# One transformer block on one core: gate and up products token-major, K chunks summed into PSUM, adaLN spans of 1024 columns, two store queues, a new order

## The chip, the cores and the metric

The kernel runs on one core of one Trainium2 chip. A core has TensorE (PE: matrix products into PSUM), VectorE (DVE), ScalarE (ACT), GpSimd (POOL) and SyncE (SP, which here only issues DMAs). The metric is the device time of one execution in microseconds. The kernel before takes 1223.05 us, the median of three runs (1222.06, 1223.05 and 1223.63).

## The reference, cut to what matters

One layer on 256 tokens of width 2048, all in fp32. `c` is one conditioning vector; the six adaLN vectors come out of one matrix-vector product with a 2048 x 12288 matrix.

```python
c_act = jax.nn.silu(c)
mod = c_act @ ada_w[l] + ada_b[l]
sh1, sc1, g1, sh2, sc2, g2 = jnp.split(mod, N_MOD, axis=-1)
h = rms_norm(x, mix_pre_g[l]) * (1.0 + sc1[:, None, :]) + sh1[:, None, :]
y = hybrid_mixer(h, w_in[l], conv_w[l], conv_b[l], conv_ln_g[l], conv_ln_b[l], w_out[l])
x = x + g1[:, None, :] * rms_norm(y, mix_post_g[l])
h = rms_norm(x, ffn_pre_g[l]) * (1.0 + sc2[:, None, :]) + sh2[:, None, :]
y = swiglu_ffn(h, w_gate[l], w_up[l], w_down[l])   # (silu(h @ w_gate) * (h @ w_up)) @ w_down
x = x + g2[:, None, :] * rms_norm(y, ffn_post_g[l])
```

`hybrid_mixer` multiplies h by `w_in` (2048 x 5120) to q, k, v (1024 columns each) and a, g (1024 each). u = a * sigmoid(g) goes through a causal depthwise convolution of width 31, a LayerNorm and silu; q, k, v through attention in 8 heads. Both halves side by side are multiplied by `w_out` (2048 x 2048). The FFN's inner width is 5632, in 11 groups of 512 columns.

## The kernel before, in words

**Weights.** Every weight matrix is streamed once from memory, in loads of 1 MiB (512 rows in four blocks of 128, by 512 columns) into five `raw` buffers, all issued on the SP queue (L604). Each half of a load (128 x 1024 numbers) is split in two: ScalarE rounds it to `wh` (L610), VectorE forms the rest `wl = raw - wh` (L611). There are five buffers of each. The activations are split likewise in a high and a low part, and each product is the sum of three matmuls: high x high, low weight x high, high weight x low.

**Two forms of product.** In the *side* form (L668 to L675) 128 weight columns are stationary and 256 tokens move, so it needs the high and low parts of both token tiles, and its result has channels on the partitions. In the *token-major* form (`mm`, L677 to L682) 128 tokens are stationary and 512 weight columns move; it needs one token tile alone, and its result has tokens on the partitions. A 1-MiB load takes 48 matmuls in the side form and 24 in the token-major one. Before, q, k, a, g, gate and up are of the side form, v, w_out and w_down token-major. The side form gives silu(gate)*up, called `hid`, in the layout in which w_down needs it as the stationary operand.

**PSUM and chunks.** Products accumulate in four `pa` tiles of 128 x 512, adaLN sums and transposes in four `pt` tiles. w_in, w_out, the first four gate/up groups and w_down run over their rows in several chunks. `put` (L709) copies a first chunk's result to SBUF with ScalarE (L715) and adds each later chunk's with VectorE (L717); the sum then lies in SBUF, from where sigmoid, silu, square and gain multiply read it.

**adaLN.** `ada` (L453) streams a span of columns: a load of 1 MiB is either eight matmuls of 256 columns or four of 512 on TensorE (L476), or as many multiply-adds on VectorE (L485 for the first, L487 for the rest). In the trace an fp32 matmul of this kind, of the sums (L518) and of the spreads (L512) counts twice, so that a load shows as x16 or x8 and one spread as x2. Then the 128 partial sums per column are summed by small matmuls with ones (L518), which gives shift and scale columns (L525, L529, L530), or spread over the partitions with a matmul of 512 columns for the two gates (L512), which are multiplied into the post-norm weights (L514). SC1, SH1 are the mixer's scale and shift, SC2, SH2 the FFN's, G1, G2 the gates. A span before has at most 512 columns. The first chunks of the mixer's input have two blocks of 128 channels (`chunks` 0, 2, 4, ...): `h_chunk` (L534) normalizes x (L544), transposes it on TensorE (L555), applies scale and shift (L561 on VectorE or L566 on ScalarE) and splits it (L576/L579 and L580).

**The rest.** The convolution (L759) is done per tap with ScalarE products (L788) that VectorE adds over all channels it covers (L791), for `nact` of the eight 128-channel blocks, and with multiply-adds on VectorE alone for the rest (L774). The LayerNorm (L804) uses TensorE for its sums (L811, L825). Between mixer and FFN, the residual sum is normalized and turned by TensorE transposes (L1119) in `h2_chunk` (L1113). At the end y is normalized, and VectorE adds it to x in eight pieces (L1186), each stored from the SP queue (L1187).

**Order.** A `Plan` gathers all steps as tasks with a cost, a priority (the table `pri`), dependences and buffers, and orders them once, when the program is built; each engine then executes its list in that order. The weight loads and the adaLN loads are two queues merged by the numbers `c_before`, `c_after`, `g1_before` and others. A step of `ada` marked as `a` in the table `mode` goes to TensorE or VectorE as the plan finds them free. Where the plan sees TensorE idle it puts in small *fill-in* matmuls of the identity (L422), whose results nobody reads. An engine whose next instruction waits holds all behind it.

Of the kernel before, what the change touches and what calls it, by code (L numbers as in the profile page):

```python
# [16 lines left out]
P = 128  # L17
# [271 lines left out]
class Job:  # L289
# [11 lines left out]
def block_kernel(ctx, tc, x, c, ada_w, ada_b, mix_pre_g, mix_post_g, w_in, conv_w, conv_b,  # L301
# [16 lines left out]
    hd_pool = ac_pool = t2_pool  # L318
    if CFG["uni"] < 2:
        hd_pool = Slots([sbt([P, 512], "hd%d" % i) for i in range(CFG["heads"])])  # L320
    if CFG["uni"] < 1:
        ac_pool = Slots([sbt([P, 512], "ac%d" % i) for i in range(CFG["acc"])])
    pri = CFG["pri"]
    br_pool = Slots([sbt([1, 512], "brow")])
# [14 lines left out]
        "w0": ("Q0", [P, 2, 2, 512], F32R), "w1": ("Q1", [P, 2, 2, 512], F32R), "w2": ("Q2", [P, 2, 2, 512], F32R),  # L339
        "conv": ("CV", [P, CT * (256 + HALO) + CT * 256], F32), "x1": ("CV", [P, NT, D], F32),  # L340
# [44 lines left out]
    nc.vector.memset(mhalf, -0.5)  # L385
    cpad = sbt([P, KB, 32], "cpad")
# [835 lines left out]
```

## Time and profile before

| | |
|---|---|
| median of three runs | 1223.05 us |
| the profiled execution's own time | 1223.58 us |
| its span in the profile | 1221.8 us |
| mean granted TensorE clock | 0.993 |
| busy: TensorE, VectorE, ScalarE, GpSimd | 98%, 72%, 49%, 1% |
| moved from memory | 304 MB, mean 251 GB/s |
| main matmuls: first, last | 34.5 us, 1212.2 us |
| last w_out product, first FFN product | 434.0 us, 449.0 us |

The span is the profiled execution from its first to its last instruction; 1.78 us of the execution's time lie outside it. In a row of the timeline stand the start, the duration, the engine, the line, the operation, what it writes and reads, the number of instructions joined in the row, and in brackets the idle time before it and who ended it. Durations of TensorE's matmuls overlap, so that their spacing is read from starts or from pieces of the chain. A row of the chain has a start, a duration, the engine, the tile and line. In the table of windows a stretch is followed by its length, the busy time and number of instructions of TensorE, its weight loads, VectorE, ScalarE and GpSimd, then the granted TensorE clock as a share of full speed, the DMA engines' share and the GB/s.

### The profile page before, as it was taken

The page shows a single profiled execution, that of the slowest core. Times are in us where ns is not written, and L with a number is a line of the kernel's source. Part 1 is how long each engine was busy: PE and PEld are TensorE (multiplying, and loading weights), DVE is VectorE, ACT ScalarE, POOL GpSimd, SP SyncE. Part 2 cuts the span into 40 slices and gives each one's busy share as a digit, 9 for nine tenths or more (in the row PEclk, how much of TensorE's full clock was granted, in tenths as well). Part 3 has the DMA queues.
Part 4 walks back from the last instruction along what each step waited for, and adds up shares of the span by engine and source line. Part 5 has one row for each costly group of instructions (what it writes and reads, how often), then busy time and mean ns, then how long its engine had stood idle before and what let it go on. Part 6 is the DMA issues. An engine that isn't in the chain of part 4 may idle for free.

```text
span 1221.8 us, 19898 instructions
## 1 busy us (share of the span) xinstructions
PE 1196.4 (98%) x8275; PEld 1072.2 (88%) x8275; DVE 877.6 (72%) x1121; ACT 599.7 (49%) x860; POOL 16.2 (1%) x29
## 2 busy tenths in 40 slices
PE   5999999999999989999999999999999999999997
PEld 4899799997558769999998789999988999999886
DVE  4799889999978789998788996444555455455554
ACT  3643344998965465534454344434433444444441
POOL 1000000000000010000000000000000000000000
PEclk9999999999998999999999999999999999999999
DMA  9999996558997989988558997655556555555532
GB/s 334 343 341 340 370 348 207 177 179 302 343 383 253 326 315 375 323 297 274 173 185 324 365 363 254 196 174 179 198 175 192 187 173 184 195 173 179 200 104 69
DMA packets 160507, 307.71 MB, mean 252 GB/s; under 512 B 5244, under 2 KB 21920, under 8 KB 159648
## 3 DMA queue, kind: packets, MB, share of 16 engines
q1 hardware_dynamic: 159520, 304.11, 72.5%
q0 software_dynamic: 544, 2.11, 0.5%
q8 instruction: 65, 1.06, 0.4%
q10 hardware_dynamic: 352, 0.21, 0.1%
q14 instruction: 26, 0.21, 0.0%
HBM read 304.32 MB, written 2.10 MB: 251 GB/s over the span
## 4 chain that ended last, share of the span: by engine, by line
PE 89%; ACT 4%; DMA 3%; DVE 1%; issue 1%; SPq 1%; POOL 0%; POOLq 0%; DVEq 0%; ACTq 0%
PE pa L674 54%; PE pa L680 10%; PE pa L682 10%; PE pa L681 10%; PE pt L476 3%; DMA raw<-in_ada_w_dram 2%; ACT prod L788 2%; ACT wh L610 1%; PE pt L518 1%; DMA xt<-in_x_dram 1%; DVE t L487 1%; PE pt L512 1%; SPq L626 0%; DVE wl L611 0%; PE pt L825 0%
## 5 line engine op out<-in xcount | busy, mean ns | idle before, releaser
L674 PE MATMUL pa<-h,wh 128*128 128x256 f32 x3840 | 701.6, 284 | 0.0
L611 DVE TENSOR_TENSOR wl<-raw,wh 128x1024 fp32r<-128x1024 f32 x372 | 451.3, 1223 | 271.8 <-ACT wh L610 270.8
L610 ACT ACTIVATE wh<-raw 128x1024 fp32r<-128x1024 f32 x372 | 392.6, 1060 | 498.0 <-PE pa L674 291.1
L674 PEld LDWEIGHTS pa<-h,wh 128*128 128x128 f32 x3840 | 593.9, 188 | 6.4 <-issue 2.7
L674 PE MATMUL pa<-h,wl 128*128 128x256 f32 x1920 | 540.9, 282 | 0.0
L674 PEld LDWEIGHTS pa<-h,wl 128*128 128x128 f32 x1920 | 363.9, 190 | 0.5 <-issue 0.2
L487 DVE SCALAR_TENSOR_TENSOR t<-raw,cact,t 128x512 f32<-128x512 f32 (+1 forms) x238 | 160.9, 676 | 7.6 <-DVE stats L832 0.3
L680 PE MATMUL pa<-wh,hid 128*128 128x512 f32 x352 | 140.9, 400 | 0.0
L682 PE MATMUL pa<-wh,hid 128*128 128x512 f32 x352 | 139.6, 397 | 0.0
L681 PE MATMUL pa<-wl,hid 128*128 128x512 f32 x352 | 139.6, 397 | 0.0
L681 PEld LDWEIGHTS pa<-wl,hid 128*128 128x128 f32 x352 | 66.4, 189 | 16.5 <-issue 0.7
L680 PEld LDWEIGHTS pa<-wh,hid 128*128 128x128 f32 x352 | 66.4, 189 | 16.5 <-issue 0.7
L682 PEld LDWEIGHTS pa<-wh,hid 128*128 128x128 f32 x352 | 66.4, 189 | 16.1
L788 ACT ACTIVATE prod<-conv,taps 128x256 f32<-128x256 f32 x180 | 74.9, 504 | 0.2 <-DVE conv L791 0.2
L791 DVE TENSOR_TENSOR conv<-conv,prod 128x1536 f32<-128x1536 f32 x30 | 52.6, 1753 | 2.1 <-ACT prod L788 1.9
L476 PE MATMUL pt<-raw,cpad 128*32 128x512 f32 (+1 forms) x384 | 45.7, 571 | 5.5 <-DMA raw<-in_ada_w_dram 5.4
L476 PEld LDWEIGHTS pt<-raw,cpad 128*32 128x32 f32 x384 | 9.1, 114 | 21.7 <-issue 10.0
L680 PE MATMUL pa<-wh,mixa 128*128 128x512 f32 x64 | 28.0, 438 | 0.0
L680 PE MATMUL pa<-wh,h 128*128 128x512 f32 x64 | 26.9, 421 | 0.0
L682 PE MATMUL pa<-wh,mixa 128*128 128x512 f32 x64 | 26.3, 412 | 0.0
L681 PE MATMUL pa<-wl,mixa 128*128 128x512 f32 x64 | 26.3, 410 | 0.0
L774 DVE SCALAR_TENSOR_TENSOR conv<-conv,taps 128x256 f32<-128x256 f32 x60 | 25.7, 480 | 0.0
(154 smaller groups left out, 786.5 us busy)
## 6 DMA issues: line engine op xcount, KB each, us to landing
raw<-in_ada_w_dram SPq DMA_DIRECT2D x96, 1024.0 KB, 7.4
raw<-in_w_gate_dram SPq DMA_DIRECT2D x44, 1024.0 KB, 5.3
raw<-in_w_up_dram SPq DMA_DIRECT2D x44, 1024.0 KB, 5.2
raw<-in_w_down_dram SPq DMA_DIRECT2D x44, 1024.0 KB, 5.1
raw<-in_w_in_dram SPq DMA_DIRECT2D x32, 1024.0 KB, 6.8
raw<-in_w_out_dram SPq DMA_DIRECT2D x16, 1024.0 KB, 7.9
raw<-in_w_in_dram SPq DMA_DIRECT2D x16, 512.0 KB, 7.4
xt<-in_x_dram SPq DMA_DIRECT2D x2, 1024.0 KB, 10.1
```

Of the source, the lines that this page charges most:

```text
L476: nc.tensor.matmul(ps.t[32 * (k % 4):32 * (k % 4) + 32, 0:wd], cpad[:, k0 + k, :], view()[:, k, :], start=me == mine[0] and k < 4, stop=me ...
L487: nc.vector.scalar_tensor_tensor(acc.t[:, 0:wd], view()[:, k, :], s, acc.t[:, 0:wd], op0=ALU.mult, op1=ALU.add)
L512: a = add("PE", 0.86, min(prio, pri["cap"]), lambda: nc.tensor.matmul(pt.t, ones, acc.t, start=True, stop=True), [a], [pt, acc])
L610: a = add("ACT", 0.475 * m, p, lambda raw=raw, u=u, m=m, wh=wh: nc.scalar.activation(wh.t[:, 0:m, :], raw.t[:, u:u + m, :], AF.Copy), [loa ...
L611: b = add("DVE", 0.567 * m, p, lambda raw=raw, u=u, m=m, wh=wh, wl=wl: nc.vector.tensor_sub(wl.t[:, 0:m, :], raw.t[:, u:u + m, :], f32(wh. ...
L674: nc.tensor.matmul(job.ps[t].t[:, 256 * n:256 * n + 256], w.t[:, j, cs], h, start=u == 0 and j == r and n == 0 and i == 0, stop=end and j ...
L680: nc.tensor.matmul(job.ps[t].t, hi, wh.t[:, j, :], start=u == 0 and j == r, stop=False)
L681: nc.tensor.matmul(job.ps[t].t, hi, wl.t[:, j, :], start=False, stop=False)
L682: nc.tensor.matmul(job.ps[t].t, lo, wh.t[:, j, :], start=False, stop=end and j == r + len(ks) - 1)
L774: nc.vector.scalar_tensor_tensor(cacc[:, k, :], upad[:, k, i:i + 256], w, cacc[:, k, :], op0=ALU.mult, op1=ALU.add)
L788: nc.scalar.activation(T("prod")[:, i % 2, k, :], upad[:, k, i:i + 256], AF.Copy, scale=w)
L791: pa = add("DVE", 0.267 * CFG["nact"] + 0.07, pri["conv"] + 0.001 * i, lambda i=i: nc.vector.tensor_add(cacc[:, nv:], cacc[:, nv:], T("pro ...
```

## The change

1. Gate and up are token-major. ScalarE applies silu to the gate's PSUM tile, VectorE multiplies it with up's PSUM tile into `z`, and four TensorE transposes (L1083 of the new kernel) for each group and token tile bring it into `hid`'s layout, after which it is split.
2. Chunk sums are formed in PSUM: VectorE adds the earlier chunks' sum in SBUF to the PSUM tile, in place (L755), and then the next step reads PSUM: a ScalarE copy to SBUF (L777) if more chunks follow, else sigmoid, silu, square, or the multiply with a, up or the gain.
3. An adaLN span may have 1024 columns, with two accumulators (or one PSUM tile in two halves) and two sums. The mixer's chunks become 2, 2, 4, 4, 4 blocks; G1, SC2 and SH2 have spans of 512, 512 and 1024 columns.
4. The side form's three products run in the order wh x high, wh x low, wl x high.
5. The numbers that set the order are other ones: priorities, the adaLN modes, chunks and cuts, where adaLN loads are merged in (G1 and the second shift and scale much earlier), `nact` 5 for 6, staggering of the last units. w_in's groups run as 8, 6, 9, 7 (g, a, g, a) where it was 6, 8, 7, 9.
6. Of the eight final stores, four are issued from the SP queue and four from ScalarE's.

```diff
+ 'nact': 5,
+ 'chunks': (0, 2, 4, 8, 12, 16),
+ 'cuts': ((0, 8, 16), (0, 2, 4, 8, 12, 16), (0, 4, 16)),
...
+        nc2 = max(1, n // 4)
+        wd = P * min(n, 4)
         per = 16 // n
-        acc = Buf(ac_pool)
+        acc = [Buf(t2_pool) for _ in range(1 if mode == "p" else nc2)]
...
-                        for i, (w, h) in enumerate(((wh, hi), (wl, hi), (wh, lo))):
+                        for i, (w, h) in enumerate(((wh, hi), (wh, lo), (wl, hi))):
...
+            if job.base is not None and not CFG["inj"]:
+                for t in range(NT):
+                    place, deps = job.base(t)
+                    last[i][t] = add("DVE", 0.602, 0.0, lambda job=job, t=t, place=place: nc.vector.tensor_add(job.ps[t].t, place(), job.ps[t].t),
+                                     deps + [last[i][t]], [job.ps[t]])
             job.evac(job, last[i])
...
-    def put(dst, job, last, first, prio=0.0, more=()):
...
+    def put(dst, job, last, prio=0.0, more=()):
+
+        return [add("ACT", 0.48, prio, lambda t=t: nc.scalar.activation(dst(t), job.ps[t].t, AF.Copy), [last[t]] + list(more), [job.ps[t]]) for t in range(NT)]
...
-                a = add("ACT", 0.61, 0.1, lambda t=t, o=o: nc.scalar.activation(job.ps[t].t, d(t), AF.Square, scale=ROOT, accum_out=stats[:, o:o + 1]), [put_[t]], [job.ps[t]])
-                b = add("DVE", 0.602, 0.15, lambda t=t: nc.vector.tensor_mul(d(t), d(t), gain[:, 512 * cg:512 * cg + 512]), [a, gdep[cg]])
+                a = add("ACT", 0.61, 0.1, lambda t=t, o=o: nc.scalar.activation(T(junk)[:, t, :], job.ps[t].t, AF.Square, scale=ROOT, accum_out=stats[:, o:o + 1]), [last[t]], [job.ps[t]])
+                b = add("DVE", 0.69, 0.15, lambda t=t: nc.vector.tensor_mul(d(t), job.ps[t].t, gain[:, 512 * cg:512 * cg + 512]), [last[t], gdep[cg]], [job.ps[t]])
...
-                    a = add("DVE", 0.602, 0.0, lambda t=t, z=z: nc.vector.tensor_mul(z.t, z.t, job.ps[t].t), [last[t], ga], [job.ps[t], z])
+                a = add("DVE", 0.69, 0.0, lambda t=t, z=z: nc.vector.tensor_mul(z.t, z.t, job.ps[t].t), [last[t], ga], [job.ps[t], z])
+
+                pt = Buf(pt_pool)
+
+                def turn(z=z, pt=pt):
+                    for k in range(4):
+                        nc.tensor.transpose(pt.t[:, P * k:P * k + P], z.t[:, P * k:P * k + P], ident)
+                a = add("PE", 0.434, pri["turn"], turn, [a], [z, pt])
...
-            weights(w_gate, 0, 512 * g, list(range(KB)), Job(pa_pool, h2_stat, h2_deps, gate_evac(g), True))
-            weights(w_up, 0, 512 * g, list(range(KB)), Job(pa_pool, h2_stat, h2_deps, up_evac(g, slot), True))
+            weights(w_gate, 0, 512 * g, list(range(KB)), Job(pa_pool, h2_stat, h2_deps, gate_evac(g)))
+            weights(w_up, 0, 512 * g, list(range(KB)), Job(pa_pool, h2_stat, h2_deps, up_evac(g, slot)))
...
-                nc.sync.dma_start(out[P * t:P * t + P, sl], T("x1")[:, t, sl])
+                (nc.scalar if i % 2 else nc.sync).dma_start(out[P * t:P * t + P, sl], T("x1")[:, t, sl])
```

The numbers given as costs in `add` calls are the plan's own and no measured times.

More of the change, by code (lines that the diff above doesn't have):

```diff
@@ L462, in ada, with all_pe @@
         parts = []
+        def all_pe():
+            return all(x.eng == "PE" for x in parts)
         for k0 in range(0, KB, per):
@@ new lines, in bias, with spread @@
+            def bias():
+                for h in range(nc2):
+                    x = acc[0 if all_pe() else h].t[64 * h:64 * h + 1, :]
+                    nc.vector.tensor_add(x, x, br.t[64 * h:64 * h + 1, :])
+            def spread():
+                for h in range(nc2):
+                    if all_pe() and nc2 == 2:
+                        nc.tensor.matmul(pts[h].t, sel[:, h:h + 1].to_broadcast([P, P]), acc[0].t, start=True, stop=True)
+                    else:
+                        nc.tensor.matmul(pts[h].t, ones, acc[h].t, start=True, stop=True)
@@ new lines, in ada @@
+            a = add("DVE", 0.602 * nc2, prio, bias, [a], [br] + acc)
+            a = add("PE", 0.86 * nc2, min(prio, pri["cap"]), spread, [a], pts + acc)
+            ends = []
+            for h in range(nc2):
+                g = gain[:, P * c0 + 512 * h:P * c0 + 512 * h + 512]
+                ends.append(add("DVE", 0.602, prio, lambda g=g, h=h: nc.vector.tensor_mul(g, g, pts[h].t), [a] + list(deps0), [pts[h]]))
+            return ends
+        pt = Buf(pt_pool)
+        def sums():
+            for j in range(min(n, 4)):
+                if all_pe() and nc2 == 2:
+                    nc.tensor.matmul(pt.t[:, 2 * j:2 * j + 2], acc[0].t[:, P * j:P * j + P], sel, start=True, stop=True)
+                else:
+                    for h in range(nc2):
+                        nc.tensor.matmul(pt.t[:, nc2 * j + h:nc2 * j + h + 1], acc[h].t[:, P * j:P * j + P], ones[:, 0:1], start=True, stop=True)
@@ L651, in weights4 @@
         nw[0] += 1
+    begun = [[]]
     def multiply(units, job, stagger):
@@ L662, in multiply_all @@
         last = [[None] * NT for _ in pairs]
+        for i, (units, job) in enumerate(pairs):
+            if job.base is not None and CFG["inj"]:
+                for t in range(NT):
+                    place, deps = job.base(t)
+                    last[i][t] = add("ACT", 0.48, pri["base"], lambda job=job, t=t, place=place: nc.scalar.activation(job.ps[t].t, place(), AF.Copy),
+                                     deps + begun[-1], [job.ps[t]])
+            begun.append([])
+        at = len(begun) - len(pairs)
         for (i, u), t in order:
@@ L1010, in f @@
+                l = add("DVE", 0.602, pri["hid"], lambda pt=pt, part=part: nc.vector.tensor_sub(part(1), pt.t.rearrange("p (k n) -> p k n", k=4), f32(part(0))), [h], [pt])
                 HID[slot][t] = [h, l]
+                PARTD.append(last[t])
         return f
     def project(kind, j, k0, k1):
-        return Job(pa_pool, h_stat, h1_deps, (ag_evac if kind >= 3 else qkv_evac)(kind % 3, j, k0 == 0, k1 == KB), kind != 2)
+        evac, place, made = (ag_evac, ag_place, AGD) if kind >= 3 else (qkv_evac, qkv_place, QKV)
```

298 lines of the change are left out of this document (151 added, 147 removed).

## The prediction

> **What bounds the kernel now.** I read the page first (busy shares and the chain), then the critical chain by stretches, then TensorE's timeline where the chain leaves TensorE, and last the table of windows with the granted clock. A difference of 0.2%, 2.45 us here, is about what a measurement of this kernel can tell from no change.
>
> ```profile
> span 1221.8 us, 19898 instructions
> PE 1196.4 (98%) x8275; PEld 1072.2 (88%) x8275; DVE 877.6 (72%) x1121; ACT 599.7 (49%) x860; POOL 16.2 (1%) x29
> PE 89%; ACT 4%; DMA 3%; DVE 1%; issue 1%; SPq 1%; POOL 0%; POOLq 0%; DVEq 0%; ACTq 0%
> ```
>
> TensorE is the bound: 89% of the chain, 98% busy. So the change is worth what it takes from TensorE's own work, plus or minus what it does to the few stretches in which TensorE waits. Those are the first 34.6 us, single waits on adaLN loads, the turn from the mixer to the FFN (434 to 449 us) and the tail. The profiled execution took 1223.58 us, 0.53 above the median of the runs, and 1.8 of it lie around the span. I add changes to the median.
>
> **Gate and up become token-major.** The spacing of both matmul forms stands in dense stretches of the trace: the first row below is one chain piece of side-form matmuls, the next two are the first and the last of 33 token-major matmuls without a gap. The last two rows count the loads.
>
> ```profile
> 938.27 184.32 PE pa L674 x1536
> 1204.65 0.40 PE L680 MATMUL pa<-wh,hid 128*128 128x512 f32 x1
> 1212.15 0.39 PE L682 MATMUL pa<-wh,hid 128*128 128x512 f32 x1
> raw<-in_w_gate_dram SPq DMA_DIRECT2D x44, 1024.0 KB, 5.3
> raw<-in_w_up_dram SPq DMA_DIRECT2D x44, 1024.0 KB, 5.2
> ```
>
> 184.32 / 1536 = 0.1200 us for 256 moving columns; (1212.15 - 1204.65) / 32 = 0.2344 us for 512. Each of the 88 loads fed 48 side matmuls (4224 in all) and will feed 24 token-major ones (2112): 2112 x 0.2344 - 4224 x 0.1200 = 495.1 - 506.9 = **-11.8 us**. Against it stand the new transposes, four for each of 11 groups and two token tiles. The trace has the same work for the FFN's input, four 128x128 transposes in one chain piece:
>
> ```profile
> 450.64 0.44 PE pt L1119 x4
> ```
>
> 22 x 0.44 = **+9.7 us**, all on TensorE. So the large rewrite is worth only -2.1 us, and the small stretches decide.
>
> Where the transposes stand in TensorE's order decides whether they wait. The following is TensorE in the middle of the FFN, after: `t_2` and `t_1` are the two token tiles' products silu(gate)*up, `h_0`/`h_1` the high and low parts of the FFN input.
>
> ```order
> L741 MATMUL pa_85<-wh_69,h_1_3832 128x512
> L739 MATMUL pa_84<-wh_71,h_0_3828 128x512
> L740 MATMUL pa_84<-wl_76,h_0_3828 128x512
> L741 MATMUL pa_84<-wh_71,h_1_3832 128x512
> L739 MATMUL pa_84<-wh_71,h_0_3828 128x512
> L740 MATMUL pa_84<-wl_76,h_0_3828 128x512
> L741 MATMUL pa_84<-wh_71,h_1_3832 128x512
> L1083 MATMUL pt_88<-ident,t_2_80 128x128 x4
> L1083 MATMUL pt_89<-ident,t_1_79 128x128 x4
> L739 MATMUL pa_85<-wh_71,h_0_3828 128x512
> ```
>
> and before, at such a place, the matmuls run on with nothing between them:
>
> ```order
> L674 MATMUL pa_84<-h_0_3834,wh_68 128x256
> L674 MATMUL pa_84<-h_0_3834,wl_73 128x256
> L674 MATMUL pa_84<-h_1_3837,wh_68 128x256
> L674 MATMUL pa_85<-h_0_3834,wh_68 128x256
> L674 MATMUL pa_85<-h_0_3834,wl_73 128x256
> L674 MATMUL pa_85<-h_1_3837,wh_68 128x256
> ```
>
> Between the last matmul of an up product and its transposes stand six matmuls, 6 x 0.2344 = 1.41 us. In that time VectorE must multiply the PSUM tile by silu(gate) (0.68 us by the add rows quoted below) and hand it over. The cover holds if VectorE comes to it at once, and not if a weight split of 1.22 us has just begun there; half of 11 groups late by some 0.1 us is **+0.5** (0 to +5, all of them late by half a microsecond).
>
> **The start.** The second adaLN chunk, columns (2,4), is the step I weigh most. Before, the first chunk (0,2) feeds a, g, q, k and v. After, a and g are cut at 8, and chunk (0,2) feeds only q, k and v: 48 side and 12 token-major matmuls, 5.8 + 2.8 = 8.6 us. VectorE takes three of the chunk's four loads. Its order from the end of the first chunk's h to the end of the second's, first before, then after (`t_1`/`h` the input, `raw` a load, `wl` a weight's low part, `s` and `b` the scale and shift):
>
> ```order
> L529 TENSOR_TENSOR s_125<-pt_88,adab 128x2
> L530 SCALAR_TENSOR_TENSOR s_125<-s_125,cols 128x2
> L611 TENSOR_TENSOR wl_74<-raw_64,wh_69 128x1024
> L485 TENSOR_SCALAR t_0_78<-raw_63,cact 128x256
> L487 SCALAR_TENSOR_TENSOR t_0_78<-raw_63,cact,t_0_78 128x256 x7
> L487 SCALAR_TENSOR_TENSOR t_0_78<-raw_65,cact,t_0_78 128x256 x8
> L611 TENSOR_TENSOR wl_75<-raw_66,wh_70 128x1024
> L611 TENSOR_TENSOR wl_76<-raw_66,wh_71 128x1024
> L525 TENSOR_TENSOR b_126<-pt_89,adab 128x2
> L611 TENSOR_TENSOR wl_77<-raw_67,wh_72 128x1024
> L579 CAST h_243<-t_1_79 128x512
> L580 TENSOR_TENSOR h_249<-t_1_79,h_243 128x512
> ```
>
> ```order
> L505 SCALAR_TENSOR_TENSOR t_2_80<-raw_65,cact,t_2_80 128x256 x7
> L660 TENSOR_TENSOR wl_75<-raw_66,wh_70 128x1024
> L521 TENSOR_TENSOR t_2_80<-t_2_80,pt_88 128x256
> L503 TENSOR_SCALAR t_0_78<-raw_67,cact 128x256
> L505 SCALAR_TENSOR_TENSOR t_0_78<-raw_67,cact,t_0_78 128x256 x7
> L578 TENSOR_TENSOR s_129<-pt_87,adab 128x2
> L579 SCALAR_TENSOR_TENSOR s_129<-s_129,cols 128x2
> L505 SCALAR_TENSOR_TENSOR t_0_78<-raw_63,cact,t_0_78 128x256 x8
> L660 TENSOR_TENSOR wl_76<-raw_64,wh_71 128x1024
> L660 TENSOR_TENSOR wl_77<-raw_65,wh_72 128x1024
> L574 TENSOR_TENSOR b_130<-pt_88,adab 128x2
> L628 CAST h_274<-t_1_79 128x512
> ```
>
> Before, VectorE had two of the four loads here and the scale stood first; after, three loads, and scale and shift both come out of them. The rows of these instructions in the trace of before, and the windows of the same stretch:
>
> ```profile
> 32.85 0.42 DVE L580 TENSOR_TENSOR h<-t,h 128x256 fp32r<-128x256 f32 x1
> 34.53 0.58 PE L674 MATMUL pa<-h,wh 128*128 128x256 f32 x1
> 40.22 1.07 PE L476 MATMUL pt<-raw,cpad 128*32 128x256 f32 x16
> 45.58 7.78 DVE L487 SCALAR_TENSOR_TENSOR t<-raw,cact,t 128x256 f32<-128x256 f32 x15
> 53.28 2.36 DVE L611 TENSOR_TENSOR wl<-raw,wh 128x1024 fp32r<-128x1024 f32 x2
> 55.74 1.02 ACT L566 ACTIVATE t<-pt,b,s 128x256 f32<-128x256 f32 x2 [0.70 <-DVE b L525]
> 56.79 0.43 DVE L579 CAST h<-t 128x512 fp32r<-128x512 f32 x1
> 57.25 0.69 DVE L580 TENSOR_TENSOR h<-t,h 128x512 fp32r<-128x512 f32 x1
> 28.00:30.00 2.00, 0.61 (x4) 0.37 (x4) 1.71 (x4) 0.52 (x2) 1.92 (x3) 0.87 1.09 364
> 34.00:36.00 2.00, 2.00 (x15) 1.47 (x8) 1.54 (x2) 0.23 (x1) 0.00 (x0) 0.50 0.83 244
> 36.00:38.00 2.00, 2.00 (x18) 2.00 (x18) 0.00 (x0) 0.60 (x1) 0.00 (x0) 0.93 1.03 357
> 44.00:52.00 8.00, 8.00 (x69) 8.00 (x69) 7.47 (x15) 4.29 (x8) 0.00 (x0) 1.00 1.06 378
> 436.00:440.00 4.00, 2.69 (x21) 1.23 (x24) 3.56 (x6) 1.44 (x3) 3.26 (x2) 1.00 1.03 376
> ```
>
> One load of eight 256-column steps is 7.78 x 8 / 15 = 4.15 us. VectorE then goes from 33.3: 4.15 + 1.2 (split) + 0.5 (add; estimate between the rows of 0.43 and 0.69) + 2 x 4.15 + 0.4 (s) + 2.4 + 0.2 (b) + 1.0 (ScalarE) + 0.4 + 0.7, so the second h is there at 52.4. TensorE starts at 34.5, has 8.6 us of main work, loses 0.9 while the clock is still half (to 36.3, since 36 to 38 has 0.93) and spends 0.4 on four transposes: it is out of main work at 44.4, and until 52.4 has two adaLN loads of 1.0 each and about 1 of sums and fill-ins, which leaves 5. Before, TensorE was busy for 8.00 of 8.00 us in 44 to 52. I take **+4** (0 to +9: 0 if VectorE's splits, whose weights come later, slip behind it, 9 if each load lands 1 to 2 us late), 1 below the working because not every split in this chain has its weight ready so early. Two adaLN loads fewer on TensorE (39 for 41 by the order) go from the time ahead of the first main matmul, dead time: 0. The other order of the three products is as many matmuls: 0.
>
> In this stretch the granted clock matters too. In the slice 28 to 30 TensorE is busy 0.61 of 2.00, the mean clock is 0.87, and it is 0.50 at 34 to 36: half from 29.5 to 36.3, 6.8 us. At 436 to 440, busy 2.69 of 4.00, it stays 1.00. The new hole would be busy about 3 of 8, nearer the first; fill-ins spread over it may hold the clock, so the sum holds nothing for it and a rival does. The Trainium skill (TensorE: Matmul & The Clock Gate, section What's actually happening) says that the clock goes to half after an idle window of about 3.4 us and comes back after a busy one, and so speaks against opening a hole. By that rule the restart would lose 1.7 us, an estimate of one window at half speed, and the sum would be +3.1. The trace agrees with the fall and the return; no row here has a clean idle window of that length.
>
> **The rest of w_in, and w_out.** Chunk sums now end in PSUM: an add of the same size there, then a ScalarE copy (122 for 52 by the order) before the tile comes free.
>
> ```profile
> L717 DVE TENSOR_TENSOR ag<-ag,pa x24: 680/683/690, 86.1 to 210.5; 128x512 f32<-128x512 f32 x24
> L715 ACT ACTIVATE ag<-pa x8: 577/598/602, 37.0 to 49.2; 128x512 f32<-128x512 f32 x8
> L788 ACT ACTIVATE prod<-conv,taps 128x256 f32<-128x256 f32 x180 | 74.9, 504 | 0.2 <-DVE conv L791 0.2
> L774 DVE SCALAR_TENSOR_TENSOR conv<-conv,taps 128x256 f32<-128x256 f32 x60 | 25.7, 480 | 0.0
> 200.00:360.00 160.00, 158.85 (x1032) 125.43 (x1030) 154.25 (x218) 143.68 (x309) 1.46 (x3) 1.00 0.74 261
> PE pt L476 <- DMA raw<-in_ada_w_dram: 5.4, 6, 1.6
> 322.50 1.07 PE L476 MATMUL pt<-raw,cpad 128*32 128x512 f32 x8 [0.29 <-DMA raw<-in_ada_w_dram]
> 331.83 1.06 PE L476 MATMUL pt<-raw,cpad 128*32 128x512 f32 x8 [0.60 <-DMA raw<-in_ada_w_dram]
> 424.96 1.06 PE L476 MATMUL pt<-raw,cpad 128*32 128x512 f32 x8 [1.11 <-DMA raw<-in_ada_w_dram]
> ```
>
> The add costs VectorE the same. Thirty copies of 0.60 less in ScalarE's conv products (150 for 180 at 0.50) and seventy more of 0.60 elsewhere add 27 us to ScalarE, which has 51% free; one more conv channel of eight on VectorE adds 30 x 0.48, less what the narrower wide adds save. TensorE lost 1.1 us in 200 to 360, where VectorE was busy 154 of 160, so both hide unless a PSUM tile comes free late (a rival). The gate G1 and the second shift and scale now load during w_in, ahead of w_out. That takes the three waits of w_out away, 0.29 + 0.60 + 1.11: **-2.0** (-2 to +1, if the convolution's output is late instead). In w_in the same loads share five buffers with the weights: **+0.5** (0 to +5; the longest such wait in the trace is 1.6).
>
> **Turn to the FFN and tail.**
>
> ```profile
> 434.36 1.06 PE L476 MATMUL pt<-raw,cpad 128*32 128x512 f32 x8
> 436.74 1.07 PE L476 MATMUL pt<-raw,cpad 128*32 128x512 f32 x8 [0.67 <-DMA raw<-in_ada_w_dram]
> 443.04 1.07 PE L476 MATMUL pt<-raw,cpad 128*32 128x512 f32 x8 [1.56 <-DMA raw<-in_ada_w_dram]
> 448.96 0.37 PE L674 MATMUL pa<-h,wh 128*128 128x256 f32 x1
> 677.16 0.86 PE pt L512 x2
> 1212.58 0.69 DVE L717 TENSOR_TENSOR y<-y,pa 128x512 f32<-128x512 f32 x1 [0.19 <-PE pa L682]
> ```
>
> Of the 14.6 us from 434.36 to 448.96 a token-major gate could save the wait for the second token tile (it needs one tile's h only), some 3 us at most. But VectorE's order now has the second tile's add ahead of the first's last one, and two adaLN loads still stand ahead: **0** (-3 to +3). At the end, one gain spread of 0.86 stands behind the last main matmul, which comes that much earlier, and its multiply (0.68, as the add) ahead of the first tile's last product. Two store queues for one give some 0.2 back: **+0.5** (-0.5 to +1.5).
>
> Sum: -11.8 + 9.7 + 0.5 + 4 - 2.0 + 0.5 + 0 + 0.5 = +1.4, and 1223.05 + 1.4 = 1224.4 us.
>
> **The rivals.** *Faster, about 1217:* VectorE's chain at the start is covered and the gate product starts on the first tile: without the 4 and with -3 at the turn the sum is -5.6, 1217.4. For it: TensorE never waited in 44 to 52 before. Against it: the order above, in which no main matmul is left to cover. Chance 0.28. *Slower, by the clock, about 1230:* the hole is the full 5 and drops the clock to half, as at 28 to 36. It lasted 6.8 us there, so main work loses 3.4: 1224.4 + 1 + 3.4 = 1228.8; if the turn falls too, 3.4 more, and I take 1230 between. It decides from a busy share between 0.61/2.00 and 2.69/4.00. Chance 0.18. That is also the rule of the page named above. *Slower, by PSUM, about 1230:* with four accumulators, a tile is held by add and copy (0.68 + 0.60, twice over two tiles, 2.6 us) where the next pair of a two-block chunk takes 2.9; with VectorE full, 60 of the 110 adds late by 0.1 give +6. Chance 0.11.
>
> **How the numbers follow.** My forecast, about no change, has 0.43, in its own range 1220.5 to 1228, of which 0.30 lies within 0.2% (1220.6 to 1225.5), 0.08 below and 0.05 above. Faster: 0.28 + 0.08 = 0.36; same 0.30; slower: 0.18 + 0.11 + 0.05 = 0.34. The range, 1214 to 1231, takes in the three other cases up to where 0.05 is left out below (turn and start both at their best) and 0.12 above (two falls of the clock, or PSUM and clock together).
>
> **What would show it.** Right: gate and up rows at 0.2344, 22 pieces of transposes of 0.44, TensorE idle for 4 to 5 us between 44 and 53, no adaLN wait in w_out, gate's start 14 to 15 us after the last w_out matmul. Wrong: TensorE waiting for VectorE ahead of the transposes, PSUM waits in w_in, a granted clock of 0.50 after 52, or main work that runs through at 44 to 52.

## The result and the profile after

| | before | after |
|---|---|---|
| median | 1223.34 us (4 runs, 1222.06 to 1223.89) | 1215.78 us (4 runs, 1214.77 to 1216.30) |
| profiled execution, its span | 1223.58, 1221.8 us | 1215.37, 1212.8 us |

The ratio is 0.9939, with a 95% interval of 0.9921 to 0.9956: the kernel became 7.6 us faster, where the prediction had 1224.4 us and "about no change" as the likeliest case. The page of after, first the span, busy shares, clock and chain:

```profile
span 1212.8 us, 15869 instructions
PE 1187.8 (98%) x6233; PEld 973.4 (80%) x6233; DVE 872.1 (72%) x1125; ACT 625.3 (52%) x904; POOL 13.8 (1%) x28
PEclk9899999999999999999999999999999999999999
PE 90%; DVE 3%; ACT 2%; DMA 2%; issue 1%; POOL 0%; ACTq 0%; DVEq 0%; POOLq 0%; SPq 0%
```

TensorE is the bound as before, with the same idle share. So the time must come out of TensorE's own work. These are the windows of two stretches in after, full of token-major matmuls, the first of gate, up and w_down, the second of w_down alone, and then of one of w_down in before (the figure in the first brackets is the number of matmuls, one or two of them cut at the edges):

```profile
645.00:757.00 112.00, 112.00 (x482) 90.11 (x481) 83.22 (x92) 45.96 (x48) 1.46 (x3) 1.00 0.85 300
1118.00:1200.00 82.00, 82.00 (x354) 66.49 (x354) 42.72 (x44) 31.91 (x40) 0.56 (x1) 1.00 0.36 117
```

```profile
1124.00:1210.00 86.00, 86.00 (x368) 69.25 (x368) 44.24 (x46) 33.78 (x43) 0.94 (x1) 1.00 0.35 122
```

Taking 1.5 off each count, the spacing is 112 / 480.5 = 0.2331 and 82 / 352.5 = 0.2326 us after, 86 / 366.5 = 0.2347 before, each good to about 0.0005 (the prediction's two rows gave 0.2344). The code of w_down did not change and the granted clock is 1.00 in all three. Yet the same matmul comes every 0.233 us instead of every 0.234. The side form, which w_in still has, shows it too, in pieces of after's chain:

```profile
111.40 21.48 PE pa L733 x180
175.26 28.80 PE pa L733 x240
```

21.48 / 180 = 0.1193 and 28.80 / 240 = 0.1200, against 0.1200 in the long pieces of before and up to 0.1204 in its short ones. After has 3744 token-major matmuls (the 2112 of gate and up, and 1632 of v, w_out and w_down, whose code is as before) and 1536 side ones. With the former some 0.0014 shorter (5 us) and the latter some 0.0007 (1 us), this is most of the 7.6 us. Neither the prediction's sum nor any of its rivals has such a term. The other places that the prediction names, TensorE's timeline of after at the start, the turn and the end, and its piece of transposes:

```profile
43.31 1.50 PE L429 MATMUL pt<-ident 128*128 128x128 f32 x12
45.53 1.06 PE L492 MATMUL pt<-raw,cpad 128*32 128x512 f32 x8 [0.72 <-DMA raw<-in_ada_w_dram]
47.23 0.61 PE L560 MATMUL pt<-ones,t 128*128 128x1 f32 x4 [0.63 <-DVE t L505]
48.59 1.94 PE L492 MATMUL pt<-raw,cpad 128*32 128x512 f32 x8
50.45 1.14 PE L429 MATMUL pt<-ident 128*128 128x128 f32 x4
51.33 0.38 PE L733 MATMUL pa<-h,wh 128*128 128x256 f32 x1
...
433.91 1.06 PE L492 MATMUL pt<-raw,cpad 128*32 128x512 f32 x8 [1.32 <-DMA raw<-in_ada_w_dram]
437.93 0.66 PE L1197 MATMUL pt<-ident,t 128*128 128x128 f32 x4 [2.10 <-ACT t L1193]
441.94 0.50 PE L739 MATMUL pa<-wh,h 128*128 128x512 f32 x1 [0.38 <-DVE h L1219]
...
1202.17 0.39 PE L741 MATMUL pa<-wh,hid 128*128 128x512 f32 x1
1202.41 1.02 PE L544 MATMUL pt<-t,ones 128*128 128x512 f32 x2
```

```profile
599.48 0.44 PE pt L1083 x4
```

The hole at the start is there: no main matmul from 43.3 to 51.3. The first product of the FFN starts at 441.9, sooner after w_out than the prediction had it. The places are those that the forecast named, and the sum over them is looked at below; the 6 us above are from somewhere else.

### The profile page after: what moved, and what is told of

It is laid out like the page before. It is cut to its first block, busy times and chain, and to the rows that moved or that the text cites. A ratio compares the mean times of both kernels' runs of the same rounds, so it can differ in the third digit from the quotient of the medians.

```text
span 1212.8 us, 15869 instructions
## 1 busy us (share of the span) xinstructions
PE 1187.8 (98%) x6233; PEld 973.4 (80%) x6233; DVE 872.1 (72%) x1125; ACT 625.3 (52%) x904; POOL 13.8 (1%) x28
## 4 chain that ended last, share of the span: by engine, by line
PE 90%; DVE 3%; ACT 2%; DMA 2%; issue 1%; POOL 0%; ACTq 0%; DVEq 0%; POOLq 0%; SPq 0%
PE pa L739 24%; PE pa L741 23%; PE pa L740 23%; PE pa L733 14%; PE pt L492 2%; DVE t L505 1%; ACT prod L857 1%; DMA raw<-in_ada_w_dram 1%; DMA xt<-in_x_dram 1%; PE pt L560 1%; PE pt L1083 1%; DMA gain<-in_conv_ln_b_dram 0%; DVE x L1184 0%; ACT wh L659 0%; PE pt L544 0%
## 5 line engine op out<-in xcount | busy, mean ns | idle before, releaser
L660 DVE TENSOR_TENSOR wl<-raw,wh 128x1024 fp32r<-128x1024 f32 x376 | 456.7, 1223 | 274.4 <-ACT wh L659 273.9
L739 PE MATMUL pa<-wh,h 128*128 128x512 f32 x768 | 306.0, 398 | 0.4 <-DVE h L1219 0.4
L741 PE MATMUL pa<-wh,h 128*128 128x512 f32 x768 | 303.3, 395 | 0.0
L740 PE MATMUL pa<-wl,h 128*128 128x512 f32 x768 | 303.1, 395 | 0.0
L733 PE MATMUL pa<-h,wh 128*128 128x256 f32 x1024 | 188.3, 285 | 0.2 <-DVE h L629 0.2
L739 PEld LDWEIGHTS pa<-wh,h 128*128 128x128 f32 x768 | 144.5, 188 | 35.6 <-issue 1.7
L741 PEld LDWEIGHTS pa<-wh,h 128*128 128x128 f32 x768 | 144.4, 188 | 34.6 <-DVE h L1220 0.4
L733 PEld LDWEIGHTS pa<-h,wh 128*128 128x128 f32 x1024 | 158.2, 189 | 16.3 <-issue 13.9
L740 PEld LDWEIGHTS pa<-wl,h 128*128 128x128 f32 x768 | 144.6, 188 | 32.8
L733 PE MATMUL pa<-h,wl 128*128 128x256 f32 x512 | 144.6, 282 | 0.0
L733 PEld LDWEIGHTS pa<-h,wl 128*128 128x128 f32 x512 | 96.6, 189 | 0.0
L857 ACT ACTIVATE prod<-conv,taps 128x256 f32<-128x256 f32 x150 | 63.1, 502 | 4.2 <-DVE conv L860 4.0
L860 DVE TENSOR_TENSOR conv<-conv,prod 128x1280 f32<-128x1280 f32 x30 | 44.5, 1482 | 0.1
```

Source lines behind the costliest of these rows:

```text
L660: b = add("DVE", 0.567 * m, p, lambda raw=raw, u=u, m=m, wh=wh, wl=wl: nc.vector.tensor_sub(wl.t[:, 0:m, :], raw.t[:, u:u + m, :], f32(wh. ...
L733: nc.tensor.matmul(job.ps[t].t[:, 256 * n:256 * n + 256], w.t[:, j, cs], h, start=(job.base is None or not CFG["inj"]) and u == 0 and j == ...
L739: nc.tensor.matmul(job.ps[t].t, hi, wh.t[:, j, :], start=(job.base is None or not CFG["inj"]) and u == 0 and j == r, stop=False, skip_grou ...
L740: nc.tensor.matmul(job.ps[t].t, hi, wl.t[:, j, :], start=False, stop=False, skip_group_check=job.base is not None and bool(CFG["inj"]))
L741: nc.tensor.matmul(job.ps[t].t, lo, wh.t[:, j, :], start=False, stop=end and j == r + len(ks) - 1, skip_group_check=job.base is not None a ...
L857: nc.scalar.activation(T("prod")[:, i % 2, k, :], upad[:, k, i:i + 256], AF.Copy, scale=w)
```

## The experiments

What differs between the kernels in a stretch that has the same code? The change adds one tile, `sel`, of 8 bytes per partition, allocated ahead of the activations; the description of the change above leaves it out. By the addresses in the built programs it takes 32 bytes, and all activations stand 32 bytes higher: the FFN's input at 171520 instead of 171488, `hid` at 155136 and 138752 instead of 155104 and 138720. The weight buffers stand where they stood (`wh` from 57472, `wl` from 77952, every buffer 4096 bytes). The sizes of the kernel's tiles, each rounded up to 32 bytes, add up to the same distances. The first experiments ask whether that is all. In each, one unused tile is put in (8 columns of 4 bytes here, more for more bytes), and no instruction differs:

```diff
     mhalf = sbt([P, 2], "mhalf")
+    pad = sbt([P, 8], "pad")
```

**b_pad32**, the kernel before with 32 bytes.

> The kernel before with one unused tile of 32 bytes per partition behind mhalf: no instruction differs, but the activations (h, mix, hid) start at 171520, 155136 and 138752 bytes, as after, instead of 32 bytes lower, that is on a multiple of 64 instead of 32 past one. Theory A (the start address sets the spacing of the matmuls): spacing falls from 0.2343 to 0.2324 to 0.2333 us token-major and from 0.1200 to about 0.119 us side form; with 1632 token-major and 5760 side matmuls that is 1.5 to 3.1 plus 5 to 7.5 us, so 1223.3 goes to about 1213 to 1217. Theory B (the spacing belongs to the new code: its instructions, order of products or where they wait): spacing stays 0.2343 and 0.1200, time 1223 within 0.2%.

Measured 1211.90 us, ratio 0.9923 (0.9904 to 0.9941). A chain piece of side matmuls, and the window of token-major ones at the end:

```profile
929.46 182.28 PE pa L675 x1536
```

```profile
1114.00:1200.00 86.00, 86.00 (x372) 69.73 (x371) 44.89 (x48) 33.04 (x41) 0.94 (x1) 1.00 0.34 119
```

0.1187 us (182.28 / 1536) and 0.2321. Theory A holds: an unused tile of 32 bytes makes the kernel before 10 us faster, at least about as much as the whole change did (the intervals overlap).

**a_pad32**, the kernel after with 32 bytes more, which puts the activations 64 bytes past where before had them.

> The kernel after with one unused tile of 32 bytes per partition, which puts the activations back on 32 past a multiple of 64: no instruction differs. Theory A: spacing rises to 0.2343 token-major and 0.1200 side; with 3744 and 1536 matmuls 4 to 7 plus 1 to 2 us, so 1215.8 goes to about 1221 to 1225, level with before: then the rest of the change is worth nothing, as the prediction's sum of +1.4 had it. Theory B: 1215.8 stays within 0.2%.

Measured 1216.33 us (ratio to before 0.9957, 0.9941 to 0.9972).

```profile
645.00:757.00 112.00, 112.00 (x481) 90.11 (x481) 83.13 (x91) 45.77 (x49) 1.46 (x3) 1.00 0.85 298
```

0.2336, between the two. The expectation failed: a start 32 past a multiple of 64 is not what made before slow.

**b_pad96**, the kernel before with 96 bytes.

> As b_pad32 with 96 bytes: the activations start at 64 past a multiple of 512 (a multiple of 64). Theory A with 64 bytes as the grain: the same gain as b_pad32, 1213 to 1217. Theory A with a coarser grain (128 bytes or more): 1223, as before. Theory B: 1223.

Measured 1196.19 us, ratio 0.9791 (0.9770 to 0.9813).

```profile
733.11 122.96 PE pa L675 x1044
923.27 174.10 PE pa L675 x1536
```

```profile
1098.00:1184.00 86.00, 86.00 (x378) 70.56 (x377) 45.86 (x49) 34.52 (x44) 0.94 (x1) 1.00 0.36 123
```

0.1178 and 0.1133 side, 0.2284 token-major, and 26 us less where a grain of 64 bytes allowed 7 to 10. The theory needs more than an alignment. One stretch of w_down in the same run is at another level, 60 / 257.5 = 0.2330:

```profile
857.00:917.00 60.00, 60.00 (x259) 48.62 (x258) 31.50 (x30) 23.48 (x24) 0.00 (x0) 1.00 0.57 192
```

**a_wh32**, the kernel after with 32 bytes ahead of the weight buffers and 32 behind `mhalf`.

```diff
+    pad0 = sbt([P, 8], "pad0")
     raw_pool = Slots([sbt([P, 4, 512], "raw%d" % i) for i in range(CFG["raw"])], Plan.REUSE)
```

> The kernel after with the weights' buffers (raw, wh, wl) and the small accumulators moved to 32 past a multiple of 64, the activations on a multiple of 64. If what counts is the moving operand (weights in the token-major form, activations in the side form): token-major spacing goes to 0.2343 and the time to about 1221. If the stationary operand counts, or only the activations: 1215.8 stays. Theory B: 1215.8 stays.

Measured 1216.74 us (0.9959, 0.9945 to 0.9973), and 482 matmuls in the same stretch of 112 us, 0.2331. Its buffers start at other places than those of a_pad32, the *distance* from the weight buffers to the activations is the same, and so is the time. This gave the second form of the theory: the distance counts, that is the start of the activations less the start of the weight buffers. The next four were chosen to break it. In bytes modulo 256, the distance is 96 in before, 128 in after and b_pad32, 160 in a_pad32 and a_wh32, 192 in b_pad96.

**a_pad64**, distance 192, by 64 bytes.

> The kernel after with 64 unused bytes: the activations start at 171584, 155200 and 138816 bytes, the places that they have in b_pad96 (448 past a multiple of 512 from the weight buffers). Theory A2 (the distance between activations and weight buffers sets the spacing, whatever the code): token-major about 0.2290 us, side form 0.1134 to 0.1178, as in b_pad96; 3744 x 0.004 + 1536 x 0.001 to 0.005 is 16 to 22 us less, so 1194 to 1200. Theory B2 (the level is an accident of each program): no tie to b_pad96, 1212 to 1218.

Measured 1199.02 us, ratio 0.9797 (0.9776 to 0.9819).

```profile
112.11 21.31 PE pa L734 x180
174.85 27.22 PE pa L734 x240
```

```profile
645.00:757.00 112.00, 112.00 (x491) 91.98 (x490) 81.12 (x88) 46.38 (x49) 1.46 (x3) 1.00 0.85 300
```

0.1134 and 0.1184 side, 0.2288 token-major, the levels of b_pad96 in other code. The order of the three side products differs between the two kernels and makes no difference to them here.

**a_pad480**, the distance of before (352, or 96 modulo 256), by 480 bytes.

> The kernel after with 480 unused bytes: the distance of the activations from the weight buffers, taken modulo 512 bytes, is 352 as in the kernel before. Theory A2 with a period of 512 bytes: token-major 0.2343, side 0.1200, and the time is that of after plus 4 to 8, 1220 to 1224, which is before against after on equal placement. Theory A2 with another period, or B2: no such rise.

Measured 1223.58 us, ratio 1.0001 (0.9987 to 1.0015).

```profile
175.64 28.79 PE pa L734 x240
```

```profile
36.00:52.00 16.00, 13.01 (x91) 9.99 (x91) 14.21 (x29) 7.56 (x13) 0.00 (x0) 1.00 0.96 339
366.00:380.00 14.00, 14.00 (x79) 12.28 (x78) 8.95 (x14) 5.66 (x8) 0.08 (x1) 1.00 0.44 150
645.00:757.00 112.00, 112.00 (x480) 90.17 (x479) 83.35 (x91) 46.55 (x49) 1.46 (x3) 1.00 0.85 300
```

0.1200 and 0.2341, the spacings of before. On this equal ground the change is worth nothing that can be measured.

**b_both32**, the kernel before with `pad0` alone, 32 bytes ahead of the weight buffers, so that all moves and the distance stays.

> The kernel before with the weight buffers and the activations both moved by 32 bytes: start addresses as in b_pad32 for the activations, but the distance to the weight buffers as in before. Theory A2 (distance): spacing 0.2343 and 0.1200, 1222 within 0.3%. Theory A1 (the activations' own start, on a multiple of 64): 0.2324 and 0.1187, about 1212.

Measured 1222.55 us, ratio 0.9998 (0.9982 to 1.0014).

```profile
937.57 184.32 PE pa L675 x1536
```

0.1200: the activations are at the addresses of b_pad32, and nothing is gained. At this pair of placements the distance counts, and not the address.

**b_pad160**, distance 0, by 160 bytes.

> The kernel before with 160 unused bytes: the activations 64 bytes further than in b_pad96, a multiple of 512 from the weight buffers. Theory A2: a level of its own, at or below that of b_pad96 if the fall from 352 (0.2343) over 384 (0.2324) to 448 (0.2290) goes on: 1190 to 1197; or back up if 448 is the best. Theory B2: any time between 1195 and 1223.

Measured 1212.79 us, ratio 0.9903 (0.9871 to 0.9935).

```profile
930.34 184.31 PE pa L675 x1536
```

```profile
1116.00:1200.00 84.00, 84.00 (x373) 69.54 (x372) 44.93 (x47) 33.84 (x43) 0.94 (x1) 1.00 0.37 125
```

0.1200 side, the worst level, and 0.2261 token-major, the best, so the time is not the 1190 to 1197 that a fall going on would have given. The two forms have different good places, which no run before this had shown.

**a_pad128**, the kernel after at distance 0.

> The kernel after with its activations a multiple of 512 bytes from the weight buffers, as in b_pad160, where the token-major spacing was 0.2267 us and the side form's 0.1200. Theory A2: the same spacings here, so against the distance of a_pad480 3744 x (0.2343 - 0.2267) = 28 us less: 1223.6 goes to about 1195, while before, with 1632 token-major matmuls, gained 10 (1212.8 for 1222.8). The change would then be worth some 17 us on equal placement, because it turns side matmuls into token-major ones: the worth of the change depends on the placement. Theory B2 (the distance is not what counts): 1212 to 1224.

Measured 1197.83 us, ratio 0.9790 (0.9764 to 0.9815).

```profile
645.00:757.00 112.00, 112.00 (x496) 92.74 (x495) 84.72 (x93) 46.80 (x49) 1.46 (x3) 1.00 0.86 304
```

0.2265. At this distance, alone among those at which both kernels ran, the change is ahead of before, by some 15 us (1197.83 for 1212.79): 2112 x 0.2265 - 4224 x 0.1200 is -28, where the prediction had -11.8.

**a_cuts64**, a_pad64 with a first chunk for a and g.

```diff
- 'cuts': ((0, 8, 16), (0, 2, 4, 8, 12, 16), (0, 4, 16)),
+ 'cuts': ((0, 2, 8, 16), (0, 2, 4, 8, 12, 16), (0, 4, 16)),
```

> As a_pad64, but a and g keep a first chunk (0,2), as in before: cuts (0,2,8,16) for (0,8,16). This gives TensorE main work for the stretch of 44 to 52 us, in which it stood idle. Theory H (the idle stretch is worth its length, as the prediction's step had it, 4 to 5 us): 1199.0 goes to 1194 to 1196. Rival (the four more chunk sums and the loads that come earlier give it back in w_in, where VectorE is full): 1198 to 1201.

Measured 1215.42 us (0.9931, 0.9908 to 0.9954), 16 more than a_pad64. Its windows, and its waits for adaLN loads:

```profile
36.00:52.00 16.00, 16.00 (x137) 14.93 (x136) 13.90 (x30) 8.59 (x13) 0.00 (x0) 1.00 0.94 311
100.00:140.00 40.00, 38.09 (x311) 35.76 (x311) 38.05 (x54) 14.43 (x20) 0.00 (x0) 0.96 1.01 359
260.00:300.00 40.00, 36.45 (x269) 27.61 (x268) 38.96 (x63) 38.34 (x91) 0.00 (x0) 0.96 0.79 287
366.00:390.00 24.00, 24.00 (x110) 20.45 (x109) 15.74 (x24) 14.16 (x21) 1.14 (x2) 0.86 0.36 125
...
PE pt L493 <- DMA raw<-in_ada_w_dram: 7.4, 5, 2.0
```

The hole is filled (16.00 of 16.00, 13.48 in a_pad64). Then TensorE is idle at 100 to 140 (1.9, all busy in a_pad64) and at 260 to 300 (3.6 for 1.2), and the clock is 0.86 at 366 to 390 (1.00 there; the clock at this place differs between executions of the same instructions, as shown below). The first main matmul starts 2.4 us later (35.70 for 33.33), and w_out ends 15.8 later (442.2 for 426.4); from there to the last main matmul both take 760. So the whole loss lies ahead of w_out's end, where the rival had it, and is larger than it said. The plan orders everything anew for other cuts, so the run doesn't price the hole by itself; it shows that filling it in this way did not pay, and not which of these differences cost how much.

**a_pad96** and **a_pad320**, distance 224, and 448, which is 192 modulo 256.

> The kernel after with the activations 480 past a multiple of 512 from the weight buffers, between a_pad64 (448: 0.2290 and 0.1134 to 0.1178) and the multiple itself (0.2267 and 0.1200). Theory A2 with a smooth dependence: 0.227 to 0.229 token-major and 0.115 to 0.120 side, 1194 to 1200. If the levels are not in order of distance: anything between 1190 and 1224.

> The kernel after with the activations 192 past a multiple of 512 from the weight buffers, that is the place of a_pad64 (448) if the period is 256 bytes. Period 256: the spacings of a_pad64, 0.2289 and 0.1134 to 0.1178, 1197 to 1201. Period 512: another level, 1195 to 1224.

1217.66 us (0.9950, 0.9933 to 0.9968) and 1198.70 us (0.9798, 0.9765 to 0.9831). The same window, of a_pad96 and then of a_pad320:

```profile
645.00:757.00 112.00, 112.00 (x481) 89.97 (x481) 83.22 (x92) 46.64 (x48) 1.46 (x3) 1.00 0.85 299
```

```profile
645.00:757.00 112.00, 112.00 (x491) 91.90 (x490) 82.53 (x90) 46.13 (x49) 1.46 (x3) 1.00 0.85 302
```

0.2336, well above both neighbours, so the levels are not in order of distance; a smooth dependence is out. And 0.2288 as in a_pad64: by this pair the period is 256 bytes, or a part of it.

**a_pad160** and **a_pad192**, distances 32 and 64, the two places left.

> The kernel after with the activations 32 past a multiple of 256 bytes from the weight buffers, one of the two places of the period not seen yet. Theory A3 (the distance modulo 256 bytes sets the spacing): one level all through the run, not that of any neighbour by need; no value can be worked out, since the six places seen (0, 96, 128, 160, 192, 224) give 0.2267, 0.2343, 0.2324 to 0.2333, 0.2333, 0.2289 and 0.2333 without a slope. Between the best and the worst: 1197 to 1224. Theory B: the spacing changes from stage to stage.

> The same with 64 past a multiple of 256 bytes, the last place not seen. 1197 to 1224. If multiples of 64 are the good places (0: 0.2267, 192: 0.2289, but 128: 0.2324 to 0.2333), then below 0.2324 and under 1212; if not, 0.2333 or more and 1214 to 1224.

1216.07 us (0.9938, 0.9920 to 0.9956) and 1214.49 us (0.9939, 0.9912 to 0.9966). In both, 482 matmuls in the stretch of 112 us, 0.2331. Distance 64 is not like 192, so the period is 256 bytes and not 128. The place of after, 128, is an ordinary one; that of before was the worst of the eight.

**a_split**, two distances in one program: h at 192, mix and hid at 0.

```diff
     mhalf = sbt([P, 2], "mhalf")
+    pad = sbt([P, 32], "pad")
...
     s1, b1, s2, b2 = (sbt([P, KB], n) for n in ("s1", "b1", "s2", "b2"))
+    T("xt"), T("ag")
+    pad2 = sbt([P, 48], "pad2")
```

> The kernel after with two distances at once: the mixer's and the FFN's input h at 192, mix and hid at 0 (multiples of 256 bytes plus that). Theory A3, each matmul by its own two operands: side form as in a_pad64 (0.1134 to 0.1178), token-major with h 0.2289, token-major with mix or hid 0.2267 as in a_pad128; 1440 x 0.0022 = 3.2 less than a_pad64, 1195 to 1197. If one distance sets the spacing for the whole program: all token-major at 0.2289 or all at 0.2267.

Measured 1194.84 us, ratio 0.9772 (0.9744 to 0.9800).

```profile
172.58 27.22 PE pa L736 x240
```

```profile
645.00:757.00 112.00, 112.00 (x494) 92.44 (x493) 80.86 (x87) 45.91 (x49) 1.47 (x3) 1.00 0.85 301
1098.00:1180.00 82.00, 82.00 (x363) 67.91 (x363) 43.68 (x45) 32.95 (x41) 0.56 (x1) 1.00 0.37 120
```

0.1134 side with h at 192; token-major 0.2268 in the second window, which is w_down with hid at 0, and 0.2274 in the first, where 191 of the 492 matmuls read h at 192. The distance acts on each matmul by its own two operands. (The lowest median; its interval overlaps with those of a_pad64, a_pad128 and b_pad96.)

**b_split**, the kernel before with the same two distances (`pad` of 40 columns).

> The kernel before with the two distances of a_split: h at 192 past a multiple of 256 bytes from the weight buffers, mix and hid at 0. Theory A3: side form 0.1134 to 0.1178 as in b_pad96, token-major with mix and hid 0.2267 as in b_pad160; 1440 x 0.0022 = 3.2 less than b_pad96, so 1192 to 1195, level with a_split or up to 3 below it: the change itself is worth nothing at this placement either. If the rewrite is worth something on equal ground: a_split is ahead, b_split at 1197 or more.

Measured 1196.47 us, ratio 0.9795 (0.9776 to 0.9815).

```profile
735.69 118.35 PE pa L677 x1044
919.33 180.91 PE pa L677 x1536
```

```profile
1102.00:1186.00 84.00, 84.00 (x373) 69.55 (x372) 44.96 (x48) 33.41 (x42) 0.94 (x1) 1.00 0.36 124
```

Token-major 0.2261 as expected. The long side piece stood at 0.1178, where b_pad96 had 0.1133 for it: 1536 x 0.0044 = 7 us lost. The piece of 1044 went the other way, 0.1134 for 0.1178, and gained 5, so the two together took 2 of the expected 3. The same code at the same distance thus has both levels, in other pieces. The intervals of a_split and b_split overlap, so here too the change is worth nothing that can be told.

All eight distances, by the runs above (token-major and side spacing in us, token-major by windows such as those shown, the side form by chain pieces of 180 matmuls or more, of which the short ones read up to 0.0006 high; a range where stages or runs differed), and the medians:

| distance mod 256 | token-major | side | before's code | after's code |
|---|---|---|---|---|
| 96 | 0.2341 to 0.2347 | 0.1199 to 0.1206 | 1223 | 1223.58 |
| 128 | 0.2321 to 0.2331 | 0.1187 to 0.1200 | 1211.90 | 1215.78 |
| 160 | 0.2331 to 0.2336 | 0.1173 to 0.1187 | | 1216.33, 1216.74 |
| 192 | 0.2284 to 0.2288, one stretch 0.2330 | 0.1133 to 0.1184 | 1196.19 | 1199.02, 1198.70 |
| 224 | 0.2336 | 0.1183 to 0.1189 | | 1217.66 |
| 0 | 0.2261 to 0.2265 | 0.1199 to 0.1206 | 1212.79 | 1197.83 |
| 32 | 0.2331 | 0.1167 to 0.1173 | | 1216.07 |
| 64 | 0.2331 | 0.1178 to 0.1184 | | 1214.49 |

## Why the prediction was wrong, step by step

**The step that failed** is the first one, as the prediction put it: "2112 x 0.2344 - 4224 x 0.1200". It took the spacing of the token-major form in the kernel before as that of the kernel after, and for the same reason it put the time of all matmuls that both kernels have (1632 token-major and 1536 side ones) at no change. The spacings of before belong to a distance of 96 between weight buffers and activations, and the change moved that to 128 by 32 bytes, by the new tile `sel`. What the runs showed in its place: at 128, each token-major matmul is some 0.0014 us shorter and each side one some 0.0007, 3 us in the step's own 2112 and another 3 in the unchanged code. By a_pad480, which is after put back to the old distance, the whole is between 7 and 8 us (ratios 1.0001 and 0.9939), that is all of the gain.

**The sum held on equal ground.** It had +1.4 us at the spacings of before. a_pad480, the code of after at those spacings, has a ratio of 1.0001 (0.9987 to 1.0015), that is +0.1, from -1.6 to +1.8. Part of that is luck, since not all parts of it stand:

- *Transposes*: 0.44 us each piece, no wait ahead of them in after's trace; the cover of 1.41 us held, and the 0.5 for late ones was nothing. Right.
- *The hole at the start*: no main matmul for 8.0 us (43.3 to 51.3 in after), 3.0 of them two adaLN loads (1.06, and 1.94 at half clock) and about 0.5 sums: 4.5, much of it spent on fill-ins, where the step had worked out 5 and took 4 (its chain on VectorE adds up to 52.55, not 52.4). At full clock, in a_pad480, it is 5.4 (8.1 from 42.7 to 50.8, less loads of 2.1 and sums of 0.6). Right. Before, in the window of a_pad480 above, TensorE was busy for all of it. The rows of before are followed by one each of b_both32, a_pad480 and after, which the next two items need:

```profile
36.00:52.00 16.00, 16.00 (x141) 15.28 (x141) 9.02 (x18) 8.35 (x13) 0.00 (x0) 0.99 1.06 361
366.00:380.00 14.00, 14.00 (x69) 12.18 (x69) 10.38 (x20) 3.65 (x7) 0.72 (x1) 0.76 0.85 298
364.00:378.00 14.00, 14.00 (x85) 12.23 (x84) 13.10 (x25) 6.29 (x10) 0.72 (x1) 1.00 0.90 322
538.00:542.00 4.00, 4.00 (x12) 3.13 (x11) 2.01 (x4) 3.08 (x9) 0.00 (x0) 0.57 1.02 360
374.00:388.00 14.00, 14.00 (x75) 12.12 (x74) 9.01 (x15) 9.04 (x17) 0.72 (x1) 0.88 0.24 78
```

- *w_out*: the step took 2.0 for three waits, and neither after nor a_pad480 has an adaLN wait left there. What that is worth can't be told from these traces, of one execution each. In before's, the clock falls behind the 32 small matmuls of the column sums (0.76 over 366 to 380: half for 6.7 us, 3.4 us of work lost). In b_both32, the same instructions at the same distance, it doesn't (1.00), and w_out ends at 428.8 for 434.0. In after it falls too, a little later (0.88 over 374 to 388), and in a_pad480 it doesn't (1.00 over 366 to 390). So the end of w_out in a_pad480, 431.7, lies between those of two executions of before's instructions, where the steps up to there add up to +2.5.
- *The turn*: one of the prediction's signs of being right failed here. It had the gate's start 14 to 15 us after the last w_out matmul, and the gate starts on the first token tile, 10.7 us after it (441.94; in before 14.9, at 448.96). Of the 4.2 us, 2.5 come back as sums and transposes that now stand between the gate's matmuls (443.7 to 446.2), which leaves about 1.7 where the step had 0.
- *The rest of the FFN*: from w_out's end to the last main matmul it is 777.7 us in a_pad480, and 778.1 in before but 782.7 in b_both32. The steps (-11.8 + 9.7 + 0 + 0.5) have -1.6, which lies between the two differences; a_pad480 also loses 1.7 us to the clock in the middle of gate and up (0.57 over 538 to 542). So the traces agree with the steps, and are no finer test of them than some 5 us.
- *Tail*: from the last main matmul's start to the span's end 10.6 us after (1202.17), 9.65 before, +1.0, of which 0.86 is the spread that was moved there; this leaves +0.1, and the step had +0.5.

**The rivals.** The faster one named about the right time, 1217, and that was luck: its gate does start on the first tile, but the hole that it counted out stayed, and the 7 to 8 us are from the spacing. The clock did fall in the hole in after (0.79 over 44 to 52) and not in a_pad480 (1.00), with the same order of instructions; where it fell it cost little (one adaLN load of 1.94 us for 1.07), since the stretch had no main work anyway. So the busy share alone, from which the prediction let it decide, doesn't settle it. The rule of the Trainium skill (TensorE: Matmul & The Clock Gate, section What's actually happening), half clock after an idle window of about 3.4 us, isn't tested here either: between the first main matmul and the last no run has a clean gap of that length, the longest being 3.08 us (a_pad480, ahead of its transposes at 438.5, with a clock of 0.50 over 440 to 442). No wait for an accumulator in PSUM is among TensorE's waits of after.

What stays open: what in the machine makes the distance count; which of two levels a stretch gets at distance 192, in the side form (0.1133 or 0.1178 to 0.1184) and in one run token-major (0.2284 or 0.2330); and what sets where the clock falls in an execution.

## What to carry to other kernels

Before a duration of the old trace is multiplied with the new kernel's counts, compare the addresses of the tiles in both programs: a new small tile ahead of the operands can shift the rate of every matmul. When a kernel is bound by TensorE, sweep the distance between its two operands' buffers in steps of 32 bytes over 256, with one unused tile; here that was worth 27 us (1223 to 1196), and the rewrite nothing that could be told at distances 96, 128 and 192 or with the two distances of the split runs, and some 15 us at distance 0. And to judge a rewrite, compare it with the old code at equal placement, as a_pad480 and b_split do, and hold a difference between stages of two traces against two executions of the same instructions first: before and b_both32 differ by 5 us in w_out's end.

## What the runs showed of the hardware

The time between two matmuls in a full stretch, at a granted clock of 1.00, goes with the distance in bytes per partition between stationary and moving operand, modulo 256: from 0.2261 to 0.2347 us for 512 moving columns and from 0.1133 to about 0.1200 for 256. The levels are not in the order of the distance (192 good, 224 poor, 0 the best for 512 columns and among the worst for 256), they moved with the distance and not with the address where the two were parted (b_both32), and they go by each matmul's own operands (a_split). The distance doesn't fix them wholly: at 192 one run has two levels in different stretches (b_pad96). The best and the worst place of the same code are 27 us apart, 2.2%. The Trainium skill (TensorE: Matmul & The Clock Gate, section Back-to-back issue gap) gives what it calls the isolated gap at full clock by the number of columns alone, N / 2.4 + 2.5 ns, which is 0.2158 us for 512 columns and 0.1092 for 256 (estimates by its formula), and for a stream with weight loads about 0.131 us at 512. The measurement decides, and no stretch here has a spacing as low as either.

The granted clock at one place differs between executions of the same instructions: behind the 32 small matmuls of the column sums it is 0.76 over 14 us in before and 1.00 in b_both32.
